# Sixteen k-tiles of an FFN's output projection as seven products of quarters, with weight sums formed by DMAs in scratch DRAM

## The chip, the cores and the metric

The kernel is one program on one core of a Trainium2 chip. The metric is device time in microseconds (us), lower is better. Engines are named as in the profile: PE (TensorE, matmuls), DVE (VectorE), ACT (ScalarE), POOL (GpSimd), SP (SyncE, which here only issues DMAs).

## The reference

A decoder trunk of two layers on 512 tokens of width 1024, in float32. Each layer has a token mixer, a cross-attention into 256 memory tokens and a SwiGLU FFN, each followed by a residual and a LayerNorm. What the change touches is the FFN, and the place where its weights are summed is the cross-attention:

```python
def swiglu(x, w_in, w_out):
    g, u = jnp.split(x @ w_in, 2, axis=-1)
    return (jax.nn.silu(g) * u) @ w_out
...
        h = layer_norm(DEEPNORM_ALPHA * h + mix, ln1_g[l], ln1_b[l])
        xa = memory_cross_attention(h, mem, w_xq[l], w_xkv[l], w_xo[l])
        h = layer_norm(DEEPNORM_ALPHA * h + xa, ln2_g[l], ln2_b[l])
        ff = swiglu(h, w_ffn_in[l], w_ffn_out[l])
        h = layer_norm(DEEPNORM_ALPHA * h + ff, ln3_g[l], ln3_b[l])
```

The hidden width of the FFN is 2816, which is 22 k-tiles of 128 for the output projection `w_out`.

## The kernel before

**Products.** Each float32 operand is kept as a high part (written by ACT, L101) and a low part (the rest, subtracted by DVE, L102). A product is three matmuls: high·high, high·low, low·high (L139 to L141). Every weight is loaded by a DMA that SP issues, in pieces of 128x1024 (512 KB), into one of four `raw` buffers, then split into a pair in `ring` or a `block`; `wchunk` (load at L125) does this for most of them.

**The FFN of one layer.** The 22 k-tiles are made in three parts of 8, 6 and 8. For each pair of k-tiles, `swiglu_seven` computes gate and up from the normalised input in seven products of quarters (a Strassen scheme; matmuls of 256 columns at L415 to L417, 168 of them per pair; only the first pair of a layer is made by `swiglu_plain`, 192 matmuls). Its weight sums are formed half by DVE and half by accumulating DMAs that POOL issues (`add_into`, L297). The result `sg` of 128x512 is split into `ph` and `pl`.

After each part, `out_proj` multiplies these k-tiles with their rows of `w_out`. For each of the four token tiles (`tt`, 128 tokens) it runs over the part's k-tiles and the two column halves of 512, three matmuls of 512 columns each, into two PSUM banks, and DVE adds the banks into the residual `h[tt]` (L286). The tile framework interleaves the matmuls of neighbouring token tiles.

**The end of a layer.** In the last part, each token tile is normalised as soon as it is complete, all on DVE: statistics (L290), mean and variance (L186, L188), subtract and scale (L192), a Newton iteration on 128x1 values (L149 to L162), scale and shift (L198). In layer 0, PE then transposes the tile (`lt_ln`, L206), ACT and DVE split it into `hT_ln`, and the next layer's first projection `pp_c` begins; it is computed in two halves, the first of which needs token tiles 0 and 1, the second tiles 2 and 3. Its weights `w_c` are split by DVE too. In layer 1, the tiles are stored instead, and the last token tile is computed in columns of 512, 256 and 256.

**Order.** Each engine runs its instructions in a fixed order, which the tile framework sets when the kernel is built, by simulating a timeline and by priorities (`tc.high_priority`). SP's DMAs stand in a queue of their own, where an issue waits until its buffer is free.

## Time and profile before

| | |
|---|---|
| median of 3 runs | 1428.9 us (1426.16 to 1429.18) |
| the profiled execution | 1427.96 us, of which the span of the trace is 1426.0 us |
| PE | 98% of the span busy, 8949 matmuls |
| DVE / ACT / POOL | 73% / 43% / 11% busy |
| the FFN of layer 0 | from 387.0 us to 722.7 us of the span |

The share of an engine is an average over the whole program; which engine ends a stretch is read from the rows of that stretch. The end of a matmul is modelled in the trace, and matmuls overlap, so the spacing of their starts says how fast PE goes.

### The profile page before, as it was taken

To read this page: it belongs to the slowest core of one execution; us is meant where nothing else is said; L and a number is where in the kernel's file an instruction comes from. 1 tells how busy PE (TensorE), PEld (TensorE's weight loads), DVE (VectorE), ACT (ScalarE), POOL (GpSimd) and SP (SyncE) were. 2 spreads that over 40 slices of the span, in tenths; PEclk is the share of its full clock that TensorE was granted. 3 is DMA by queue.
4 is the path that set the end of the run, shared out by engine and by line. 5 is a ranking of instruction groups with operands and counts; after the bars stand their busy time and mean duration, and the time that the engine had idled before them with its cause. 6 is when DMAs were issued, how large, how long until landed. Compare 5 with 4: busy or idle time off the path is not lost.

```text
span 1426.0 us, 22119 instructions
## 1 busy us (share of the span) xinstructions
PE 1396.7 (98%) x8949; PEld 1251.3 (88%) x8949; DVE 1034.0 (73%) x1701; ACT 608.0 (43%) x977; POOL 151.4 (11%) x98
## 2 busy tenths in 40 slices
PE   7998989999999999999999999999999999999997
PEld 6787888988899899899897889889889998989996
DVE  6699978656886376576769999685678764756667
ACT  5552461442456055255136235524525632534540
POOL 2373330000010000000013200000000000000000
PEclk9999999999999999999999999999999999999999
DMA  7522242322265364465242235512215663545531
GB/s 253 152 63 90 86 151 71 105 70 92 75 163 148 104 155 126 122 167 155 77 124 89 74 114 168 163 59 89 78 42 142 165 181 75 137 144 134 163 104 60
DMA packets 109306, 168.63 MB, mean 118 GB/s; under 512 B 7548, under 2 KB 82000, under 8 KB 109204
## 3 DMA queue, kind: packets, MB, share of 16 engines
q1 hardware_dynamic: 103156, 145.99, 31.9%
q0 software_dynamic: 5760, 20.97, 7.8%
q8 instruction: 70, 1.15, 0.3%
q14 instruction: 32, 0.26, 0.1%
q10 hardware_dynamic: 288, 0.26, 0.1%
HBM read 144.13 MB, written 2.10 MB: 103 GB/s over the span
## 4 chain that ended last, share of the span: by engine, by line
PE 85%; DVE 6%; issue 3%; ACT 3%; POOL 2%; DMA 1%; SPq 0%; DVEq 0%; POOLq 0%; ACTq 0%
PE po_fo L140 6%; PE po_fo L139 6%; PE po_fo L141 6%; PE fx L417 5%; PE fx L415 5%; PE fx L416 5%; PE fw L416 3%; PE fw L417 3%; PE fw L415 3%; DVE cv L611 3%; PE pp_xq L139 2%; PE pp_xq L140 2%; PE pp_xq L141 2%; PE po_xo L141 2%; PE po_xo L139 2%
## 5 line engine op out<-in xcount | busy, mean ns | idle before, releaser
L611 DVE SCALAR_TENSOR_TENSOR cv<-u,chan,cv 128x511 f32<-128x511 f32 (+29 forms) x240 | 159.6, 728 | 0.2
L140 PE MATMUL po_fo<-w_fo,ph 128*128 128x512 f32 (+1 forms) x360 | 138.2, 385 | 0.0
L141 PE MATMUL po_fo<-w_fo,pl 128*128 128x512 f32 (+1 forms) x360 | 137.6, 385 | 0.0
L297 POOL DMA_DIRECT2D s<-raw_a x40 | 34.8, 873 | 952.9 <-PE pp_f L141 473.8
L139 PE MATMUL po_fo<-w_fo,ph 128*128 128x512 f32 (+1 forms) x360 | 132.0, 385 | 0.0
L101 ACT ACTIVATE w_a<-raw_a 128x1024 fp32r<-128x1024 f32 x60 | 63.2, 1055 | 135.6 <-PE po_fo L141 110.2
L102 DVE TENSOR_TENSOR w_s<-s,w_s 128x1024 fp32r<-128x1024 f32 x80 | 97.3, 1220 | 28.3 <-ACT w_s L101 28.1
L101 ACT ACTIVATE w_s<-s 128x1024 fp32r<-128x1024 f32 x80 | 83.8, 1053 | 46.6 <-DMA s<-raw_a 33.6
L286 DVE SCALAR_TENSOR_TENSOR h<-h,po_fo 128x512 f32<-128x512 f32 (+1 forms) x49 | 32.6, 674 | 90.6 <-PE po_fo L141 90.6
L417 PE MATMUL fx<-T_ln,w_s 128*128 128x256 f32 x320 | 90.6, 283 | 0.0
L416 PE MATMUL fx<-T_ln,w_s 128*128 128x256 f32 x320 | 90.6, 283 | 0.0
L415 PE MATMUL fx<-T_ln,w_s 128*128 128x256 f32 x320 | 90.6, 283 | 0.0
L102 DVE TENSOR_TENSOR w_a<-raw_a,w_a 128x1024 fp32r<-128x1024 f32 x60 | 73.2, 1220 | 11.7 <-ACT w_a L101 10.5
L141 PEld LDWEIGHTS po_fo<-w_fo,pl 128*128 128x128 f32 x360 | 67.7, 188 | 13.2
L140 PEld LDWEIGHTS po_fo<-w_fo,ph 128*128 128x128 f32 x360 | 67.7, 188 | 13.0
L139 PEld LDWEIGHTS po_fo<-w_fo,ph 128*128 128x128 f32 x360 | 67.3, 188 | 12.9
L102 DVE TENSOR_TENSOR w_fo<-raw_fo,w_fo 128x1024 fp32r<-128x1024 f32 x44 | 52.9, 1219 | 16.2 <-ACT w_fo L101 16.2
L415 PEld LDWEIGHTS fx<-T_ln,w_s 128*128 128x128 f32 x320 | 61.4, 192 | 0.0
L416 PEld LDWEIGHTS fx<-T_ln,w_s 128*128 128x128 f32 x320 | 61.4, 192 | 0.0
L417 PEld LDWEIGHTS fx<-T_ln,w_s 128*128 128x128 f32 x320 | 61.4, 192 | 0.0
L140 PE MATMUL pp_xq<-hT_ln,w_xq 128*128 128x256 f32 (+1 forms) x192 | 61.3, 322 | 0.0
L139 PE MATMUL pp_xq<-hT_ln,w_xq 128*128 128x256 f32 (+1 forms) x192 | 60.0, 320 | 0.5 <-ACT hT_ln L101 0.5
(317 smaller groups left out, 4420.5 us busy)
## 6 DMA issues: line engine op xcount, KB each, us to landing
raw_a<-w_ffn_in SPq DMA_DIRECT2D x60, 512.0 KB
raw_fo<-w_ffn_out SPq DMA_DIRECT2D x44, 512.0 KB
s<-raw_a POOLq DMA_DIRECT2D x40, 512.0 KB, 5.1
s<-w_ffn_in SPq DMA_DIRECT2D x20, 512.0 KB
raw_xv<-w_xkv SPq DMA_DIRECT2D x16, 512.0 KB
raw_c<-w_in SPq DMA_DIRECT2D x16, 512.0 KB
...
```

Source lines behind the costliest of these rows:

```text
L101: ACT.activation(hi, src, AF.Copy)
L102: eng.tensor_sub(lo, src, f(hi))
L139: PE.matmul(o, lh, rh, start=start, stop=False)
L140: PE.matmul(o, lh, rl, start=False, stop=False)
L141: PE.matmul(o, ll, rh, start=False, stop=stop)
L286: DVE.scalar_tensor_tensor(h[tt][:, c0:c1], h[tt][:, c0:c1], scale, bks[c][:, :c1 - c0], ALU.mult, ALU.add)
L297: POOL.dma_start(dst, src, accum_op=ALU.add)
L415: PE.matmul(o, wh, bh, start=start and k == 0, stop=False, skip_group_check=True)
L416: PE.matmul(o, wh, bl, start=False, stop=False, skip_group_check=True)
L417: PE.matmul(o, wl, bh, start=False, stop=stop and k == 3, skip_group_check=True)
L611: DVE.scalar_tensor_tensor(cv[ct][:, s:], u[:, ct, :T - s], wj, cv[ct][:, s:], ALU.mult, ALU.add)
```

## The change

The parts become 8, 8 and 6 k-tiles. The first two, 16 k-tiles, use a new `out_proj_seven`; the last keeps `out_proj`, with its LayerNorms.

`out_proj_seven` takes the 8 k-tiles of a part as 4 pairs and splits the product into quarters: k-tiles of even and odd place, token halves of 256, column halves of 512. Seven products replace eight. Each is 2 token tiles x 4 pairs x 3 = 24 matmuls of 512 columns, 168 for a part where 192 stood. In place of two banks per token tile there are three pairs of banks (X, W, Y), and each product (for X, the growing sum) is added to or subtracted from the quarters of `h` where it belongs: 14 adds of 128x512 by DVE for each part instead of 8.

The moving side needs sums of quarters of `sg`: the class `PairQuads` lets DVE form T1 to T4 (256 columns wide) for each pair and splits them, in place of the plain split. The weight side needs four sums, S1 to S4. Each is formed in scratch DRAM, in two halves of 512 KB: SP issues a copy of one quarter of `w_out`, and POOL an accumulating DMA on top of it. In all, 14 operands of 512 KB are loaded and split for each part, where 8 were.

The 16 copies and 16 accumulating DMAs of a layer are put into the cross-attention: a list `aside` holds them, and each `wchunk` load there (8 of `w_xq`, 8 of `w_xo`) is followed in SP's queue by one copy.

```diff
+    aside = []
+
+    def behind(load):
+
+        if aside:
+            with tc.issue_after(load.ins):
+                aside.pop(0)()
+
     def wchunk(src, nk, ncol, name, resident=False, fine=False):
 
         raw = stage.tile([P, 1024], F32, tag="raw", name=f"raw_{name}")
         rv = raw.rearrange("p (k c) -> p k c", k=nk)
-        nc.sync.dma_start(rv, src.rearrange("(k p) c -> p k c", p=P))
+        behind(nc.sync.dma_start(rv, src.rearrange("(k p) c -> p k c", p=P)))
         if resident:
             w = block([P, 2, 1024], F32R, f"w_{name}")
         else:
...
-        POOL.dma_start(dst, src, accum_op=ALU.add)
+        POOL.dma_start(dst, src, accum_op=ALU.add, max_dma_last_dim=4096)
...
+    class PairQuads:
+        PLACE = {"11": (0, 4, 6, 10), "21": (1, 5, 7, 11), "22": (2, 3, 8, 9)}
+        SUMS = {"T1": 0, "T2": 1, "T4": 2, "T3": 3}
+        def __init__(self, j0, name):
+            self.j0 = j0
+            self.t = [block([P, 2, 4, 256], F32R, f"pT{i}_{name}") for i in range(4)]
+            self.b = [block([P, 2, 4, 256], F32R, f"pB{i}_{name}") for i in range(3)]
+        def get(self, n, i):
+            if n in self.SUMS:
+                t, e = self.t[i], self.SUMS[n]
+            else:
+                e = self.PLACE[n][i]
+                t, e = self.b[e // 4], e % 4
+            return t[:, 0, e, :], t[:, 1, e, :]
+        def second(self, j, sg, uu):
+            i = (j - self.j0) // 2
+            t3 = uu[1][:, 256:]
+            DVE.tensor_sub(t3, sg[1][:, 256:], sg[0][:, 256:])
+            split(*self.get("T3", i), t3)
+            split(*self.get("22", i), sg[1][:, 256:])
+        def first(self, j, sg, uu):
+            i = (j - self.j0) // 2
+            for m, n in enumerate(("11", "21")):
+                split(*self.get(n, i), sg[m][:, :256])
+            t1, t2, t4 = uu[0][:, :256], uu[0][:, 256:], uu[1][:, :256]
+            DVE.tensor_sub(t1, sg[0][:, :256], sg[0][:, 256:])
+            DVE.scalar_tensor_tensor(t2, t1, -1.0, sg[1][:, 256:], ALU.mult, ALU.subtract)
+            DVE.scalar_tensor_tensor(t4, t2, -1.0, sg[1][:, :256], ALU.mult, ALU.subtract)
+            split(self.t[i][:, 0, 0:2, :].rearrange("p e c -> p (e c)"),
+                  self.t[i][:, 1, 0:2, :].rearrange("p e c -> p (e c)"), uu[0])
+            split(*self.get("T4", i), t4)
+    def quarter_of(w, c, k, u):
+        v = w.rearrange("(q two p) c -> two p q c", two=2, p=P)
+        return v[k][:, 2 * u:2 * u + 2, c * 512:(c + 1) * 512]
+    def weight_sums(w, name):
+        s = {n: [dram.tile([P, 2, 512], F32, tag=f"{n}{u}_{name}", name=f"{n}{u}_{name}") for u in range(2)]
+             for n in ("S1", "S2", "S3", "S4")}
+        def step(n, at, plus, u):
+            nc.sync.dma_start(s[n][u], quarter_of(w, *at, u))
+            add_into(s[n][u], s[plus][u] if plus in s else quarter_of(w, *plus, u))
+        for n, at, plus in (("S3", (0, 0), (1, 0)), ("S2", (1, 1), "S3"), ("S1", (1, 0), (1, 1)), ("S4", (0, 1), "S2")):
+            for u in range(2):
+                aside.append(lambda n=n, at=at, plus=plus, u=u: step(n, at, plus, u))
+        return s
+    def out_proj_seven(w, sums, pq, name, scale):
+        A = {"11": (0, 0), "12": (0, 1), "22": (1, 1)}
+        def operand(n, u):
+            raw = stage.tile([P, 1024], F32, tag="raw", name=f"raw_{n}{u}_{name}")
+            src = sums[n][u] if n in sums else quarter_of(w, *A[n], u)
+            nc.sync.dma_start(raw.rearrange("p (k c) -> p k c", k=2), src)
+            wt = ring.tile([P, 2, 1024], F32R, tag="w", name=f"w_{n}{u}_{name}")
+            split(wt[:, 0, :], wt[:, 1, :], raw)
+            return wt
+        plan = (("S3", "T3", "W"), ("11", "11", "X"), ("12", "21", "Y"), ("S2", "T2", "X"), ("22", "T4", "W"),
+                ("S1", "T1", "X"), ("S4", "22", "X"))
+        tags = {"X": "acc", "W": "tr", "Y": "cv"}
+        ws, banks, seen = {}, {}, set()
+        for n, b, g in plan:
+            if g not in banks:
+                banks[g] = [bank(f"fo{g}{i}_{name}", tag=tags[g]) for i in range(2)]
+            ws[n] = [operand(n, u) for u in range(2)]
+        def add(t, c, g, i):
+            tt, cs = t * 2 + i, slice(c * 512, (c + 1) * 512)
+            k = scale if (tt, c) not in seen else 1.0
+            seen.add((tt, c))
+            with tc.high_priority(offset=HP):
+                DVE.scalar_tensor_tensor(h[tt][:, cs], h[tt][:, cs], k, banks[g][i], ALU.mult,
+                                         ALU.subtract if c else ALU.add)
+        reads = {"S3": (1, 1), "11": (0, 0), "12": (0, 0), "S2": (0, 1), "22": (0, 1), "S1": (1, 1), "S4": (1, 0)}
+        opened = set()
+        for n, b, g in plan:
+            bank_major = n in ("S1", "S4")
+            parts = [(i, u) for i in range(2) for u in range(2)] if bank_major else \
+                [(i, u) for u in range(2) for i in range(2)]
+            for i, u in parts:
+                for k in range(2):
+                    ph, pl = pq.get(b, u * 2 + k)
+                    ts_ = slice(i * P, (i + 1) * P)
+                    wh, wl = (ws[n][u][:, j, k * 512:(k + 1) * 512] for j in range(2))
+                    o, first = banks[g][i], (g, i) not in opened
+                    opened.add((g, i))
+                    last = n in ("S4", "22", "12") and u == 1 and k == 1
+                    PE.matmul(o, ph[:, ts_], wh, start=first, stop=False, skip_group_check=True)
+                    PE.matmul(o, ph[:, ts_], wl, start=False, stop=False, skip_group_check=True)
+                    PE.matmul(o, pl[:, ts_], wh, start=False, stop=last, skip_group_check=True)
+                if bank_major and u == 1:
+                    add(*reads[n], g, i)
+            if not bank_major:
+                for i in range(2):
+                    add(*reads[n], g, i)
...
+        quads = isinstance(dest, PairQuads)
         with tc.high_priority(offset=HP):
             for m in range(2):
                 ACT.activation(sg[m][:, hi], X[m][:, lo], AF.Silu)
+            if quads:
+                for m in range(2):
+                    DVE.scalar_tensor_tensor(sg[m][:, hi], sg[m][:, hi], -1.0, uu[m][:, hi], ALU.mult, ALU.mult)
+                dest.second(j, sg, uu)
         product(w4, t4, W, False, True)
-        out = []
         with tc.high_priority(offset=HP):
             for m in range(2):
                 DVE.tensor_add(uu[m][:, lo], W[m][:, lo], u2[m])
             for m in range(2):
-                DVE.scalar_tensor_tensor(sg[m], sg[m], -1.0, uu[m], ALU.mult, ALU.mult)
-                split(ph[:, i0 + m, :], pl[:, i0 + m, :], sg[m])
-                out.append((ph[:, i0 + m, :], pl[:, i0 + m, :]))
-        return out
+                s = lo if quads else slice(0, T)
+                DVE.scalar_tensor_tensor(sg[m][:, s], sg[m][:, s], -1.0, uu[m][:, s], ALU.mult, ALU.mult)
+            dest.first(j, sg, uu)
...
+        sums = [weight_sums(a["w_ffn_out"][l][g * NK * P:(g + 1) * NK * P, :], n_(f"fs{g}")) for g in range(2)]
...
-        for part, (j0, nj) in enumerate(((0, 8), (8, 6), (14, 8))):
-            pT = []
+        for part, (j0, nj) in enumerate(((0, 8), (8, 8), (16, 6))):
+            seven = part < 2
+            p = PairQuads(j0, n_(f"p{part}")) if seven else Pairs(j0, nj, n_(f"p{part}"))
             for j in range(j0, j0 + nj, 2):
-                if (j - j0) % 4 == 0:
-                    ph = block([P, 4, T], F32R, n_(f"ph{j}"))
-                    pl = block([P, 4, T], F32R, n_(f"pl{j}"))
-                if j == 0:
-                    pT += swiglu_plain(w_fi, quads, j, ph, pl, f"{l}")
-                else:
-                    pT += swiglu_seven(w_fi, quads, j, ph, pl, (j - j0) % 4, f"{l}")
-            norm = None
-            if part == 2:
-                gb3 = load_gb(a["ln3_g"][l], a["ln3_b"][l], n_("ln3"))
-                hT = new_hT(n_("ln3")) if l < L - 1 else None
-
-                def norm(tt, st):
-                    layer_norm(tt, st, gb3, n_("ln3"), hT,
-                               store=out[0, tt * P:(tt + 1) * P, :] if l == L - 1 else None)
-            out_proj(w_fo[j0 * P:(j0 + nj) * P, :], pT, n_(f"fo{part}"), ALPHA if part == 0 else 1.0, norm=norm,
-                     fin=part == 2 and l == L - 1)
+                (swiglu_seven if j else swiglu_plain)(w_fi, quads, j, p, f"{l}")
+            scale = ALPHA if part == 0 else 1.0
+            w_part = w_fo[j0 * P:(j0 + nj) * P, :]
+            if seven:
+                out_proj_seven(w_part, sums[part], p, n_(f"fo{part}"), scale)
+                continue
+            gb3 = load_gb(a["ln3_g"][l], a["ln3_b"][l], n_("ln3"))
+            hT = new_hT(n_("ln3")) if l < L - 1 else None
+
+            def norm(tt, st):
+                layer_norm(tt, st, gb3, n_("ln3"), hT,
+                           store=out[0, tt * P:(tt + 1) * P, :] if l == L - 1 else None)
+
+            out_proj(w_part, p.stat, n_(f"fo{part}"), scale, norm=norm, fin=l == L - 1)
```

SP's queue, at the loads of `w_xo` (`raw_xo`) in layer 0's cross-attention, before:

```order
L125 DMA raw_xo_2990<-w_xo 128x1024
L125 DMA raw_xo_2995<-w_xo 128x1024
L125 DMA raw_xo_3000<-w_xo 128x1024
L125 DMA raw_xo_3005<-w_xo 128x1024
L125 DMA raw_xo_3010<-w_xo 128x1024
```

The same place in the changed kernel (`S_fs` is a half of one of the sums):

```order
L134 DMA raw_xo_3024<-w_xo 128x1024
L460 DMA S_fs_0_2318<-w_ffn_out 256x1x512
L134 DMA raw_xo_3031<-w_xo 128x1024
L460 DMA S_fs_0_2319<-w_ffn_out 256x1x512
L134 DMA raw_xo_3038<-w_xo 128x1024
L460 DMA S_fs_0_2316<-w_ffn_out 256x1x512
```

Every load now has a copy of the same size behind it; the accumulating DMAs stand in POOL's queue.

DVE, at the end of layer 0, where the low parts of `hT_ln` are written; `lt_ln_01` is token tile 1, `h_102` and `h_103` are the rows of token tiles 2 and 3, and `w_c` are the next layer's weights. Before:

```order
L192 SCALAR_TENSOR_TENSOR h_102<-h_102,mv_ln_02_6764,gb_ln_0_6490 128x512 x2
L149 TENSOR_SCALAR y_ln_02_6770<-v_ln_02_6766 128x1
L102 TENSOR_TENSOR hT_ln_0_6495<-lt_ln_01_0_6694,hT_ln_0_6493 128x4x128
L102 TENSOR_TENSOR hT_ln_0_6496<-lt_ln_01_1_6702,hT_ln_0_6494 128x4x128
L156 TENSOR_SCALAR t_ln_02_6771<-y_ln_02_6770,v_ln_02_6766 128x1
L162 TENSOR_SCALAR y_ln_02_6770<-t_ln_02_6771,y_ln_02_6770 128x1
L156 TENSOR_SCALAR t_ln_02_6771<-y_ln_02_6770,v_ln_02_6766 128x1
L162 TENSOR_SCALAR s_ln_02_6772<-t_ln_02_6771 128x1
L286 SCALAR_TENSOR_TENSOR h_103<-h_103,po_fo_0_3_0_6795 128x512
L162 TENSOR_SCALAR y_ln_02_6770<-s_ln_02_6772,y_ln_02_6770 128x1
L290 BN_STATS st_fo_03_6845<-h_103 128x6
```

The changed kernel, from the same L192 rows of token tile 2 (there `h_104`; `h_105` is token tile 3, and the adds are at L295):

```order
L201 SCALAR_TENSOR_TENSOR h_104<-h_104,mv_ln_02_6964,gb_ln_0_6736 128x512 x2
L103 TENSOR_TENSOR hT_ln_0_6741<-lt_ln_00_0_6832,hT_ln_0_6739 128x4x128
L299 BN_STATS st_fo_03_7033<-h_105 128x6
L158 TENSOR_SCALAR y_ln_02_6970<-v_ln_02_6966 128x1
L103 TENSOR_TENSOR hT_ln_0_6742<-lt_ln_00_1_6840,hT_ln_0_6740 128x4x128
L103 TENSOR_TENSOR w_c_100_7095<-raw_c_100_7093,w_c_100_7095 128x1024
L103 TENSOR_TENSOR w_c_101_7100<-raw_c_101_7098,w_c_101_7100 128x1024
L165 TENSOR_SCALAR t_ln_02_6971<-y_ln_02_6970,v_ln_02_6966 128x1
L103 TENSOR_TENSOR w_c_110_7107<-raw_c_110_7105,w_c_110_7107 128x1024
L295 SCALAR_TENSOR_TENSOR h_105<-h_105,po_fo_0_3_1_6996 128x512
L103 TENSOR_TENSOR hT_ln_0_6741<-lt_ln_01_0_6906,hT_ln_0_6739 128x4x128
L103 TENSOR_TENSOR hT_ln_0_6742<-lt_ln_01_1_6914,hT_ln_0_6740 128x4x128
```

The low parts of token tile 1 stood ahead of the first add of token tile 3; they now stand behind its second add (the one shown) and behind three splits of `w_c`.

## Rows read from the trace of the kernel before

**Rows 1.** The page: the span, and each engine's busy time, share and instructions.
```profile
span 1426.0 us, 22119 instructions
PE 1396.7 (98%) x8949; PEld 1251.3 (88%) x8949; DVE 1034.0 (73%) x1701; ACT 608.0 (43%) x977; POOL 151.4 (11%) x98
```

**Rows 2.** Windows, layer 0's FFN: from:to, length, busy PE, PEld, DVE, ACT, POOL, clock, DMA, GB/s.
```profile
387.00:722.70 335.70, 335.60 (x2325) 314.30 (x2325) 224.34 (x300) 150.32 (x231) 18.42 (x21) 1.00 0.48 129
```

**Rows 3.** Timeline of PE inside an `out_proj`: start, duration; seven rows left out between.
```profile
480.02 0.39 PE L140 MATMUL po_fo<-w_fo,ph 128*128 128x512 f32 x1
...
482.06 0.39 PE L140 MATMUL po_fo<-w_fo,ph 128*128 128x512 f32 x1
```

**Rows 4.** Windows, the period of one pair in `swiglu_seven`.
```profile
534.00:554.16 20.16, 20.16 (x170) 20.16 (x170) 12.98 (x17) 11.53 (x20) 0.88 (x1) 1.00 0.47 129
```

**Rows 5.** Timeline of DVE within that period, idle time before a row in brackets.
```profile
543.75 0.42 DVE L462 TENSOR_TENSOR uu<-fw,u 128x256 f32<-128x256 f32 x1 [2.81 <-PE fw L417]
544.09 1.22 DVE L102 TENSOR_TENSOR w_s<-s,w_s 128x1024 fp32r<-128x1024 f32 x1
545.22 0.68 DVE L464 SCALAR_TENSOR_TENSOR sg<-sg,uu 128x512 f32<-128x512 f32 x1
545.82 0.41 DVE L462 TENSOR_TENSOR uu<-fw,u 128x256 f32<-128x256 f32 x1
```

**Rows 6.** Timeline of DVE at the end of layer 0.
```profile
692.33 1.37 DVE L286 SCALAR_TENSOR_TENSOR h<-h,po_fo 128x512 f32<-128x512 f32 x2 [5.17 <-PE po_fo L141]
...
699.28 1.41 DVE L198 SCALAR_TENSOR_TENSOR h<-h,y_ln,gb_ln 128x512 f32<-128x512 f32 x2
...
720.12 3.48 DVE L102 TENSOR_TENSOR w_c<-raw_c,w_c 128x1024 fp32r<-128x1024 f32 x3
```

**Rows 7.** Timeline of PE, the next layer's first matmul.
```profile
722.71 0.28 PE L139 MATMUL pp_c<-hT_ln,w_c 128*128 128x256 f32 x1
```

**Rows 8.** The chain that ended last, end of layer 0: start, duration, piece.
```profile
723.35 0.87 PE lt_ln L206 x8
...
736.39 0.74 PE pp_c L139 x4
```

**Rows 9.** Timeline of DVE at the end of layer 1.
```profile
1388.10 1.36 DVE L286 SCALAR_TENSOR_TENSOR h<-h,po_fo 128x512 f32<-128x512 f32 x2 [4.90 <-PE po_fo L141]
1389.38 1.28 DVE L290 BATCH_NORM_STATS2 st_fo<-h 128x6 f32<-128x512 f32 x2
...
1392.33 0.14 DVE L149 TENSOR_SCALAR y_ln<-v_ln 128x1 int32<-128x1 int32 x1
...
1394.44 0.69 DVE L286 SCALAR_TENSOR_TENSOR h<-h,po_fo 128x512 f32<-128x512 f32 x1 [0.60 <-PE po_fo L141]
...
1405.33 1.37 DVE L286 SCALAR_TENSOR_TENSOR h<-h,po_fo 128x512 f32<-128x512 f32 x2 [2.44 <-PE po_fo L141]
...
1411.44 0.69 DVE L286 SCALAR_TENSOR_TENSOR h<-h,po_fo 128x512 f32<-128x512 f32 x1 [0.37 <-PE po_fo L141]
...
1417.19 0.42 DVE L286 SCALAR_TENSOR_TENSOR h<-h,po_fo 128x256 f32<-128x256 f32 x1 [1.99 <-PE po_fo L141]
...
1421.35 1.67 DVE L198 SCALAR_TENSOR_TENSOR h<-h,y_ln,gb_ln 128x256 f32<-128x256 f32 x4
```

**Rows 10.** Timeline of SP's DMA issues in layer 0's cross-attention.
```profile
212.59 44.75 SPq L125 DMA_DIRECT2D raw_xq<-w_xq  x8
274.55 44.13 SPq L125 DMA_DIRECT2D raw_xo<-w_xo  x8
```

**Rows 11.** Timeline of ACT there, where the loads are first read.
```profile
289.00 1.06 ACT L101 ACTIVATE w_xo<-raw_xo 128x1024 fp32r<-128x1024 f32 x1 [1.75 <-issue]
...
332.26 3.92 ACT L101 ACTIVATE w_xo<-raw_xo 128x1024 fp32r<-128x1024 f32 x4
```

**Rows 12.** The page's DMA queues: packets, MB, share of 16 engines' span.
```profile
q1 hardware_dynamic: 103156, 145.99, 31.9%
q0 software_dynamic: 5760, 20.97, 7.8%
```

More of the change, by code (lines that the diff above doesn't have):

```diff
@@ L374, in swiglu_plain @@
                                 kh == 0 and k == 0, kh == 1 and k == 3)
-        out = []
         with tc.high_priority(offset=HP):
+            sg, uu = ([tmp.tile([P, T], F32, tag="t", name=f"{s}{j}{m}_{name}") for m in range(2)] for s in ("sg", "uu"))
             for m in range(2):
-                sg = tmp.tile([P, T], F32, tag="t", name=f"sg{j}{m}_{name}")
-                ACT.activation(sg, banks[0][m], AF.Silu)
-                DVE.tensor_mul(sg, sg, banks[1][m])
-                split(ph[:, m, :], pl[:, m, :], sg)
-                out.append((ph[:, m, :], pl[:, m, :]))
@@ L463, in swiglu_seven @@
             for m in range(2):
[L464 to L467 removed]
+                s = lo if quads else slice(0, T)
+                DVE.scalar_tensor_tensor(sg[m][:, s], sg[m][:, s], -1.0, uu[m][:, s], ALU.mult, ALU.mult)
+            dest.first(j, sg, uu)
     def mem_T(name):
```

20 lines of the change are left out of this document (16 added, 4 removed).

## The prediction

> **What bounds the kernel now.** I read first the page's shares: PE is busy 98% of the span, DVE 73%, the others less than half [rows 1]. Then the windows of the FFN, the stretch that the change rewrites: PE is busy for 335.6 of 335.7 us at a granted clock of 1.00, DVE for 224.3 [rows 2]. So matmuls taken out of this stretch shorten it one for one, until another engine is late. Third, the ends of the two layers, where one chain runs through LayerNorm on DVE: there I read DVE's timeline and the chain. Last, the cross-attention, where the new DMAs go: SP's issues against ACT's reads.
>
> **PE: what is removed.** A part of 8 k-tiles costs `out_proj` 4 x 8 x 2 x 3 = 192 matmuls of 512 columns, and `out_proj_seven` 7 x 24 = 168. Between two starts nine matmuls apart lie 2.04 us [rows 3]: 0.227 us each. The 24 saved are 5.44 us for a part, and four parts give 21.8 us. This is the ceiling. Dividing 22 k-tiles as 8, 8, 6 in place of 8, 6, 8 changes no other count.
>
> **DVE inside the parts.** Its prices, from the spacing of starts [rows 5]: 0.34 us for 256 columns, 1.13 for a split of 1024, 0.60 for 512. One pair's period on PE is 168 matmuls in 20.16 us, in which DVE works 12.98 [rows 4]; in other periods it also has two weight sums (estimate 2 x 1.13), so up to 15.2. Per pair the change adds three differences and one more for T3 (4 x 0.34), low parts of five pieces of 256 and one of 512 in place of two of 512 (1.7 + 0.6 - 1.2), and multiplies in halves (4 x 0.34 - 2 x 0.6): 2.6 us in all. That makes 17.8 of 20.16, so DVE fits with over 2 us left. In the row before the weight split DVE had waited 2.81 us for PE [rows 5]: such waits are the cover. Should the work come too late there, PE waits at its next bank, and nothing else hides it.
>
> For a part, `out_proj_seven` adds six more splits (6.8 us) and six adds (3.6) on DVE: 10.4 us, in a stretch of 168 x 0.227 = 38.1 us. DVE's total over the FFN rises from 224 to some 224 + 2 x 10.4 + 8 x 2.6 = 266, against 335.7 - 10.9 = 325 on PE: 82%. Each bank pair is added to `h` while PE runs another product (24 x 0.227 = 5.4 us, against 2 x 0.6 for the adds), except X from S1 to S4, where the product runs bank by bank to give half of that. For these handoffs I put 1 us over all four parts, nearer to the lower end because the adds are short beside a product; the bounds are 0 and 4.8 (the adds of one product, 1.2 us, bare once in each part).
>
> **The end of layer 0.** The last part now has 6 k-tiles, so nearly the whole saving of the layer falls after the first add of the last `out_proj`. Counted in issue order from the start of the FFN's output products, PE has run 401 matmuls at that add before (192 + 144 + 65), and 396 now (168 + 168 + 60; token tiles 0 and 1 are interleaved). So up to there only 5 x 0.227 = 1.1 us is saved. The rest, 43 matmuls or 9.7 us, should come between that add at 692.33 and the second half of `pp_c` at 736.39 [rows 6, 8]. There DVE sets the pace: until the low part of token tile 1, on which `pp_c` begins, the changed order puts eight adds, seven statistics, six and four passes of 512 columns (L192, L198), four low parts, three splits of `w_c` and two Newton chains before PE may go on. Neighbouring operations overlap by 0.08 (0.68 long, the next start 0.60 later [rows 5]), so a pair of adds of 1.37 costs 0.65 each, a pass 0.66 (1.41 for two), a split 1.13 (3.48 for three) [rows 6], a statistic 0.64 (1.28 for two) [rows 9]; a low part is 512 wide, 0.60. Eight adds 5.2, seven statistics 4.5, ten passes 6.6, four low parts 2.4, three splits 3.4, and the small operations, counted as three chains of 1.5 (1392.33 until the wait of 0.60 that ends at 1394.44 [rows 9]), 4.5: 26.6 us. PE has only 84 x 0.227 + 2 x 0.87 for transposes [rows 8] = 20.8 us to do until then. It waits 5.8 us, where before it came from the last product to `pp_c` at 722.71 without a wait [rows 7]. 9.7 - 5.8 = 3.9, and with the 1.1 **layer 0 gains 5.0 us** of its 10.9.
>
> **The end of layer 1.** From the first add at 1388.10 to the last pass (1421.35 + 1.67 = 1423.02) are 34.9 us, in which DVE waits for PE 0.60 + 2.44 + 0.37 + 1.99 = 5.4 us [rows 9]. So its own work is 29.5 us. PE after the change needs from that add 68 x 0.227 + 36 x 0.12 (a matmul of 256 columns: 20.16 / 168 [rows 4]) = 19.7 us: DVE is the longer by 10. The stretch becomes 29.5, which is 5.4 shorter; ahead of it 402 matmuls become 394, 1.8. **Layer 1 gains 7.2 us.**
>
> **Cross-attention: what is added.** SP issues eight loads of `w_xo` in 44.13 us and eight of `w_xq` in 44.75 [rows 10], 5.5 us apiece, paced by buffers coming free. From the first issue at 274.55 to ACT's read at 289.00 are 14.4 us; the last, issued by 318.7, is read as the last of four from 332.26 on, at about 335 [rows 10, 11]: slack of over 14 us. With each load now come a copy and an accumulate of 512 KB. By the queues, q0 (40 accumulates) took 7.8% of 1426 us, 2.8 us each of all 16 engines; q1 moved 145.99 MB in 31.9%, 1.6 us for 512 KB [rows 12]. Sum: 1.6 + 1.6 + 2.8 = 6.0. No row shows a copy or accumulate whose both sides lie in DRAM. Lower bound: overlap as good as no cost, below 5.5. Upper: both doubled, 1.6 + 3.2 + 5.6 = 10.4, less what is issued while loads wait. At 6.0 the queue falls 0.5 x 8 = 4 us behind within the eight loads, which the 14 us cover. I take nothing, near the rows. PE, DVE and ACT get no new work there, and POOL's 16 accumulates a layer stand on an engine that is 11% busy [rows 1].
>
> The Trainium skill, page "DMA: Bandwidth & Descriptors", section "Issuing engines are not separate DMA queues", says that DMAs of all issuing engines run on the same 16 DMA engines and interleave. By that rule, POOL's accumulates delay SP's loads though their queue is another one; it speaks against the change, and the first rival below is worked out that way. No row of before shows the two together in this stretch.
>
> **Sum.** 5.0 + 7.2 - 1 = 11.2 us. The profiled execution took 1427.96 (2 us more than its span), so 1416.8; the median of the runs is 0.9 above it. I say **1417.5**.
>
> **The rivals.**
> *The loads of cross-attention fall behind (slower).* With t us of all DMA engines for a load, a copy and an accumulate, the last `w_xo` load is late by 8 x (t - 5.5) less 12.8 of slack (14.4, a load of 1.6 us taken off). It cancels the 11.2 us, 5.6 for a layer, when t = 5.5 + 18.4/8 = 7.8. At t = 9.6, short of the upper bound, it is 20 us a layer, and the time 1417.5 + 40 = 1457.5. For it: an accumulate is nearly twice the price of a load, and a copy within DRAM is unseen. Against: slack is large, and the loads in the FFN share the DMA engines with accumulates at a share of 0.48 without PE waiting [rows 2]. Chance 0.09; from it comes most of "slower".
>
> *DVE is late inside the pairs.* 16 pair periods of `swiglu` feed `PairQuads` over both layers. If PE waits x us in each, x = 0.7 takes all the gain (1428); x = 0.35 gives 1422. The point is a DVE period over 20.2 us: 2.4 more than my 17.8. For it: the order of DVE is fixed, and a late operation holds back the next; against: waits such as 2.81 in one place [rows 5]. Chance 0.21 for 1421 to 1431.
>
> *The layer ends cost nothing.* If DVE does its late work in PE's shadow, all 21.8 us come but the 1 us: 1407. For it: the pieces of the chain at layer 0's end are PE's [rows 8]; against: the sums above. Chance 0.1 for 1406 to 1412.
>
> **How the numbers follow.** The forecast case, 1412 to 1421, holds 0.6; its width is that of the handoffs and of an error of 10% in the two sums on DVE. The range of 8 in 10 takes in part of both neighbours, 1408 to 1428; outside remain 0.04 of the third rival, 0.05 of the second and the first. A measurement tells from no change about 0.2%, that is below 1426.0 or above 1431.8. Faster: 0.6 + 0.1 + 0.1 of the second rival = 0.80; same: 0.08 of the second; slower: its remaining 0.03 and the first rival, 0.12.
>
> **What would show it.** Right: the out_proj of the first two parts shows 168 matmuls at 0.227 without gaps; PE waits some 5 to 6 us ahead of `pp_c` in layer 0, on a low part of `hT_ln`; DVE's last stretch in layer 1 has no wait for PE; `w_xo` is read on ACT as before. Wrong: PE gaps in `fw` or `fx` rows released by DVE; a gap in cross-attention ahead of `pp_xq` or `po_xo` released by ACT or a DMA; a `pp_c` that begins without a wait.

## The result and the profile after

The changed kernel took 1412.36 us (median of 4 runs, 1410.32 to 1414.95) against 1427.53 for the kernel before in the same comparison (4 runs, 1423.87 to 1429.18): a ratio of 0.9898, 95% interval 0.9871 to 0.9925, so 10.7 to 18.4 us faster. 1417.5 had been forecast, with 1408 to 1428 as range. The profiled execution is the slowest of the four runs (1414.95 us, span 1413.3); against the span of before it is 12.7 us shorter, and the accounts below go by the two profiled executions.

The page of the changed kernel, first the span and the engines, then the DMA queues (packets, MB, share of 16 engines' span), which answer to [rows 1, 12]:

```profile
span 1413.3 us, 22464 instructions
PE 1380.2 (98%) x8847; PEld 1235.4 (87%) x8847; DVE 1110.4 (79%) x1905; ACT 650.4 (46%) x1065; POOL 181.8 (13%) x130
q1 hardware_dynamic: 118388, 175.35, 38.0%
q0 software_dynamic: 12416, 37.75, 14.6%
```

Windows of the changed kernel (from:to, length, busy PE, PEld, DVE, ACT, POOL, clock, DMA share, GB/s): the FFN of layer 0, from the same matmul on as [rows 2]; a stretch of its first product of seven, with some matmuls of the neighbouring pairs; the `w_xo` loads of cross-attention.

```profile
387.72:716.10 328.38, 326.81 (x2277) 305.54 (x2276) 259.01 (x392) 170.99 (x275) 18.37 (x21) 1.00 0.54 151
467.40:503.20 35.80, 35.80 (x166) 29.95 (x165) 29.07 (x37) 14.66 (x17) 1.06 (x2) 1.00 0.70 213
276.00:321.00 45.00, 45.00 (x271) 39.89 (x269) 26.42 (x52) 22.91 (x49) 6.78 (x7) 1.00 0.96 258
```

PE has no gap in the product of seven. DVE is busy for 79% of the FFN's stretch (259.0 of 328.4). The stretch of [rows 2] does not hold the whole FFN: in the kernel before its first matmul starts at 374.4, 12.6 us ahead of the 387.0 given there, and the accounts below start with that matmul. In cross-attention the DMA engines are now nearly full, 0.96, and PE is still busy for all of it.

To place the 12.7 us, the program is cut at points that both kernels have: the first matmul of the FFN (`pp_f`), the first transpose `pc` behind the start of the second half of `pp_c` (layer 0) and the last instruction (layer 1), read from PE's timeline.

| | layer 0, `pp_f` to `pc` | layer 1, `pp_f` to the end |
|---|---|---|
| before | 374.4 to 737.1: 362.7 us | 1070.2 to 1425.9: 355.7 us |
| changed | 375.1 to 733.7: 358.6 us | 1066.5 to 1413.2: 346.7 us |
| difference | 4.1 | 9.0 |

Outside of these the difference is 0.4 us the other way. So of the 10.9 us of matmuls that a layer saves, layer 0 keeps 4.1 and layer 1 keeps 9.0.

**Layer 0's end.** PE's timeline of the changed kernel, where `pp_c` begins (start, duration, idle before and its releaser):

```profile
716.11 0.62 PE L148 MATMUL pp_c<-hT_ln,w_c 128*128 128x256 f32 x3 [0.25 <-ACT hT_ln L102]
718.21 0.39 PE L148 MATMUL pp_c<-hT_ln,w_c 128*128 128x256 f32 x1 [1.48 <-DVE h L295]
718.81 0.39 PE L149 MATMUL pp_c<-hT_ln,w_c 128*128 128x256 f32 x1 [0.21 <-DVE hT_ln L103]
```

DVE's timeline just before, with everything that PE waits for in a row:

```profile
713.89 2.35 DVE L103 TENSOR_TENSOR w_c<-raw_c,w_c 128x1024 fp32r<-128x1024 f32 x2
716.16 0.27 DVE L165 TENSOR_SCALAR t_ln<-y_ln,v_ln 128x1 f32<-128x1 f32 x1
716.35 1.21 DVE L103 TENSOR_TENSOR w_c<-raw_c,w_c 128x1024 fp32r<-128x1024 f32 x1
717.48 0.68 DVE L295 SCALAR_TENSOR_TENSOR h<-h,po_fo 128x512 f32<-128x512 f32 x1
718.08 1.28 DVE L103 TENSOR_TENSOR hT_ln<-lt_ln,hT_ln 128x512 fp32r<-128x512 f32 x2
```

The reader sees the forecast queue: three splits of `w_c`, the second add of token tile 3, and only then the low parts. The longer wait, 1.48 us, ends with that add and not with a low part: `pp_c` and `po_fo` take their PSUM banks from the same four (`BANKS` in the kernel), and `pp_c`'s next high·high matmul needs the bank that the add reads. The low part ends the shorter one; it stands right behind the add, so an earlier add alone would have freed PE for one matmul only. PE's starts lie 1.76 and 0.60 us apart at the two matmuls where 0.12 is normal: 2.1 us lost. A second price follows, which no row of before shows. Windows of the changed kernel behind this wait:

```profile
718.80:722.70 3.90, 3.89 (x20) 3.89 (x21) 3.59 (x10) 1.67 (x3) 0.00 (x0) 0.58 0.47 129
722.70:726.70 4.00, 4.00 (x35) 4.00 (x34) 3.89 (x12) 0.00 (x0) 0.00 (x0) 0.99 0.91 285
```

The granted clock is 0.58 over 3.9 us (from 719.4 on PE is at the lower of its two levels, 1.2 GHz, 0.21 us per matmul where 0.12 is normal), then full again. In 3.9 us 20 matmuls start, in the next 4.0 there are 35. Sixteen at 0.09 more are 1.5 us.

**Layer 1's end.** DVE's last stretch, as in [rows 9]; of the rows between only those are shown in which DVE waits for PE, and the start of the last chain:

```profile
1383.14 1.28 DVE L295 SCALAR_TENSOR_TENSOR h<-h,po_fo 128x512 f32<-128x512 f32 x2 [5.13 <-PE po_fo L150]
...
1389.06 0.14 DVE L158 TENSOR_SCALAR y_ln<-v_ln 128x1 int32<-128x1 int32 x1
1389.11 0.69 DVE L299 BATCH_NORM_STATS2 st_fo<-h 128x6 f32<-128x512 f32 x1
1389.71 0.26 DVE L165 TENSOR_SCALAR t_ln<-y_ln,v_ln 128x1 f32<-128x1 f32 x1
1389.88 0.20 DVE L195 BATCH_NORM_AGGREGATE mv_ln<-st_fo 128x2 f32<-128x12 f32 x1
...
1400.94 0.42 DVE L295 SCALAR_TENSOR_TENSOR h<-h,po_fo 128x256 f32<-128x256 f32 x1 [0.62 <-PE po_fo L150]
...
1403.09 0.42 DVE L295 SCALAR_TENSOR_TENSOR h<-h,po_fo 128x256 f32<-128x256 f32 x1 [0.45 <-PE po_fo L150]
...
1407.08 0.15 DVE L158 TENSOR_SCALAR y_ln<-v_ln 128x1 int32<-128x1 int32 x1
...
1408.63 1.67 DVE L207 SCALAR_TENSOR_TENSOR h<-h,y_ln,gb_ln 128x256 f32<-128x256 f32 x4
```

From the first add to the last pass 27.2 us (1383.14 to 1410.30), where before it was 34.9. The waits for PE shrank from 5.4 to 1.1. The rest, 3.4 us, is something else: now that DVE has two token tiles at hand, the small operations of one chain stand between operations of another tile (1389.06 to 1389.88), whereas the last chain, alone, still takes 1.55 us (1407.08 to 1408.63). The same stretch as windows of the kernel before:

```profile
1388.10:1423.02 34.92, 29.06 (x151) 24.85 (x149) 28.18 (x69) 0.00 (x0) 0.00 (x0) 0.97 0.13 49
```

And of the changed kernel:

```profile
1383.14:1410.30 27.16, 19.91 (x105) 17.03 (x103) 25.78 (x69) 0.00 (x0) 0.00 (x0) 0.91 0.17 62
```

69 instructions on DVE each time; 28.2 us of busy time became 25.8. Summed one by one they are hardly shorter (30.6 and 30.3 us); what grew is the time in which one overlaps the next (2.4 and 4.6 us).

**Inside the parts.** In layer 0 PE loses 3.2 us more than before ahead of the last products (the sum over the starts of what exceeds 0.227 and 0.120 us), in layer 1 0.5. In this execution it is mostly in the first part, ahead of `fx`. ACT there stands behind an accumulating DMA:

```profile
408.65 1.06 ACT L102 ACTIVATE w_s<-s 128x1024 fp32r<-128x1024 f32 x1 [4.89 <-DMA s<-raw_a]
```

But ACT's timeline of before has the same wait at the same place (33.4 us behind the FFN's first matmul, 33.5 after), and PE loses nothing there:

```profile
407.80 1.06 ACT L101 ACTIVATE w_s<-s 128x1024 fp32r<-128x1024 f32 x1 [4.77 <-DMA s<-raw_a]
```

So the late DMA alone does not make PE wait. New are the splits of `PairQuads` on ACT behind it. The longest of these waits shows one, in ACT's timeline of the changed kernel:

```profile
434.05 0.61 ACT L102 ACTIVATE pT_p<-uu 128x512 fp32r<-128x512 f32 x1
434.57 0.37 ACT L564 ACTIVATE u<-fx 128x256 f32<-128x256 f32 x1
```

And in PE's:

```profile
434.99 0.39 PE L551 MATMUL fx<-T_ln,w_s 128*128 128x256 f32 x1 [0.51 <-ACT u L564]
```

PE waits for the copy `u`, and the new split delays that copy by 0.52 us.

### The profile page after: what moved, and what is told of

It reads as the page before. It is cut to its first block, busy times and chain, and to the rows that moved or that the text cites. A ratio compares the mean times of both kernels' runs of the same rounds, so it can differ in the third digit from the quotient of the medians.

```text
span 1413.3 us, 22464 instructions
## 1 busy us (share of the span) xinstructions
PE 1380.2 (98%) x8847; PEld 1235.4 (87%) x8847; DVE 1110.4 (79%) x1905; ACT 650.4 (46%) x1065; POOL 181.8 (13%) x130
## 4 chain that ended last, share of the span: by engine, by line
PE 87%; DVE 3%; ACT 3%; issue 3%; POOL 2%; DMA 1%; SPq 0%; DVEq 0%; ACTq 0%; POOLq 0%
PE fx L551 5%; PE fx L553 5%; PE fx L552 5%; PE fw L553 3%; PE fw L552 3%; PE fw L551 3%; PE pp_xq L149 2%; PE pp_xq L148 2%; PE pp_xq L150 2%; PE foX_fo L512 2%; PE po_xo L150 2%; PE po_xo L148 2%; PE foX_fo L513 2%; PE po_xo L149 2%; PE foX_fo L514 2%
## 5 line engine op out<-in xcount | busy, mean ns | idle before, releaser
L103 DVE TENSOR_TENSOR w_s<-s,w_s 128x1024 fp32r<-128x1024 f32 x80 | 97.6, 1220 | 38.9 <-ACT w_s L102 38.7
L149 PE MATMUL pp_xq<-hT_ln,w_xq 128*128 128x256 f32 (+1 forms) x192 | 61.3, 322 | 0.0
L148 PE MATMUL pp_xq<-hT_ln,w_xq 128*128 128x256 f32 (+1 forms) x192 | 59.9, 320 | 0.5 <-ACT hT_ln L102 0.5
L150 PE MATMUL pp_xq<-hT_ln,w_xq 128*128 128x256 f32 (+1 forms) x192 | 60.4, 318 | 0.0
L102 ACT ACTIVATE hT_ln<-lt_ln 128x512 fp32r<-128x512 f32 x24 | 13.9, 595 | 97.5 <-PE lt_ln L215 97.3
L149 PE MATMUL pp_c<-hT_ln,w_c 128*128 128x512 f32 (+1 forms) x160 | 56.9, 358 | 0.2 <-DVE hT_ln L103 0.2
L148 PE MATMUL pp_c<-hT_ln,w_c 128*128 128x512 f32 (+1 forms) x160 | 55.1, 361 | 1.7 <-DVE h L295 1.5
L150 PE MATMUL pp_c<-hT_ln,w_c 128*128 128x512 f32 (+1 forms) x160 | 56.3, 354 | 0.0
L102 ACT ACTIVATE w_S_fo<-raw_S_fo 128x1024 fp32r<-128x1024 f32 x32 | 33.8, 1058 | 35.8 <-PE foX_fo L514 14.2
L149 PE MATMUL po_xo<-w_xo,oTh 128*128 128x512 f32 x128 | 49.5, 389 | 0.0
L150 PE MATMUL po_xo<-w_xo,oTl 128*128 128x512 f32 x128 | 49.4, 391 | 0.0
```

The lines of the kernel that those rows point to most:

```text
L102: ACT.activation(hi, src, AF.Copy)
L103: eng.tensor_sub(lo, src, f(hi))
L148: PE.matmul(o, lh, rh, start=start, stop=False)
L149: PE.matmul(o, lh, rl, start=False, stop=False)
L150: PE.matmul(o, ll, rh, start=False, stop=stop)
```

## The experiments

All spans are those of the profiled execution. The two stretches are cut as in the table above. What lies outside of them takes 702.8 to 708.3 us in these executions (705.3 and 703.7 in the two of one and the same kernel, with `w_c` on POOL), so not all of a difference between two spans belongs to the FFN.

| run | us, median (range) | span | layer 0 stretch | layer 1 stretch |
|---|---|---|---|---|
| split only | 1429.93 (1429.24 to 1431.24) | 1428.2 | 364.8 | 357.1 |
| one part | 1417.47 (1416.22 to 1418.22) | 1416.2 | 359.4 | 352.1 |
| 8, 6, 8 | 1419.07 (1414.95 to 1422.16) | 1415.2 | 360.0 | 352.5 |
| no token sums | 1409.82 (one run) | 1408.1 | 355.9 | 347.2 |
| no weight sums | 1412.45 (1412.01 to 1414.61) | 1410.9 | 355.1 | 349.0 |
| weight sums twice | 1440.75 (1439.46 to 1442.94) | 1441.2 | 370.3 | 364.5 |
| `w_c` on POOL | 1411.60 (1411.18 to 1412.90) | 1409.5 | 356.7 | 347.5 |
| 6, 8, 8 | 1420.24 (1419.75 to 1422.09) | 1418.0 | 361.0 | 350.9 |
| changed, again | 1413.58 (1411.00 to 1416.88) | 1415.2 | 358.0 | 348.8 |
| `w_c` on POOL, again | 1409.76 (1407.98 to 1410.52) | 1406.3 | 355.0 | 347.5 |

### The split into 8, 8, 6 alone

In the kernel before:

```diff
-        for part, (j0, nj) in enumerate(((0, 8), (8, 6), (14, 8))):
+        for part, (j0, nj) in enumerate(((0, 8), (8, 8), (16, 6))):
```

> The kernel before with its parts as 8, 8 and 6 k-tiles, all by the plain output projection: no matmul less, no sums. Theory (the last part's size decides what the end of a layer costs): the last part is 6 k-tiles as in the changed kernel, so PE waits about 3.6 us for DVE at the end of layer 0, and at the end of layer 1 DVE's stretch is 7.7 us shorter while 42 matmuls (9.5 us) more come ahead of it, 1.8 us longer. Sum: 5.4 us slower than before, a span near 1431. Rival (the loss comes with the seven products, from their adds and splits on DVE): no change, a span near 1426, and no wait of PE at pp_c.

Measured: 1.0034 of before (interval 1.0022 to 1.0046), so 3.1 to 6.6 us slower; by the stretches 2.1 in layer 0 and 1.4 in layer 1. PE's timeline at `pp_c` has the wait of the changed kernel to 0.01 us:

```profile
722.37 0.62 PE L139 MATMUL pp_c<-hT_ln,w_c 128*128 128x256 f32 x3 [0.25 <-ACT hT_ln L101]
724.47 0.38 PE L139 MATMUL pp_c<-hT_ln,w_c 128*128 128x256 f32 x1 [1.48 <-DVE h L286]
725.08 0.39 PE L140 MATMUL pp_c<-hT_ln,w_c 128*128 128x256 f32 x1 [0.22 <-DVE hT_ln L102]
```

The clock stayed at 1.00 behind it, and so layer 0 lost 2.1 and not 3.6. The theory holds: the wait comes from the last part's six k-tiles, not from the seven products. Set against this run, the products alone give 6.2 us in layer 0 and 10.4 in layer 1, of 10.9 each; the rest is what was found above, 3.2 of waits inside the parts and 1.5 of clock in layer 0, 0.5 of waits in layer 1. DVE's last stretch in layer 1 is 27.2 us here too (1398.10 to 1425.26), so its shortening comes from the split as well.

### One part by seven products

```diff
-        for part, (j0, nj) in enumerate(((0, 8), (8, 8), (16, 6))):
-            seven = part < 2
+        for part, (j0, nj) in enumerate(((0, 8), (8, 6), (14, 8))):
+            seven = part == 0
...
+            if part == 1:
+                out_proj(w_part, p.stat, n_(f"fo{part}"), scale)
+                continue
```

> The parts stay 8, 6, 8; only the first part of each layer uses the seven products (8 copies and 8 accumulates a layer in place of 16). 48 matmuls less, 10.9 us. Theory (ends cost what the last part's size makes them cost, and the first part loses 3.2 us in layer 0 and 0.5 in layer 1 inside its pairs): ends as before, 1426.0 - 10.9 + 3.7 = 1418.8 span. Rival (every part of seven products pays its own share of the loss, half of 9.1 us): 1426.0 - 10.9 + 4.5 with waits inside the pairs small and a wait at the layer end: 1419.6; the two are told apart by where PE waits, not by the time. Third, no loss: 1415.

Measured: 0.9943 of before (0.9930 to 0.9956); the stretches are 3.3 and 3.6 us shorter, of 5.4 each. `pp_c` begins without a wait, as before:

```profile
717.02 0.39 PE L150 MATMUL po_fo<-w_fo,p_p 128*128 128x512 f32 x1
717.25 0.28 PE L148 MATMUL pp_c<-hT_ln,w_c 128*128 128x256 f32 x1
```

A last part of 8 costs nothing at the end. The 2 us missing in each layer are waits ahead of `fx` in the first part (in layer 0 PE's starts there exceed the normal spacing by 0.37, 0.36 and 0.30 in single places). So the waits inside the pairs were not 3.2 and 0.5 as in the one profile of the changed kernel, but about 2 in both layers of this execution.

### Parts of 8, 6 and 8, the first two by seven products

The second part has three pairs; its second halves are 256 KB. The core of the edit:

```diff
-        for part, (j0, nj) in enumerate(((0, 8), (8, 8), (16, 6))):
+        for part, (j0, nj) in enumerate(((0, 8), (8, 6), (14, 8))):
...
+        sizes = (2, w.shape[0] // (2 * P) - 2)
...
-                for k in range(2):
+                for k in range(sizes[u]):
```

> The parts stay 8, 6, 8, and the first two use the seven products, the second with three pairs (126 matmuls in place of 144); the last part of 8 is plain. 84 matmuls less than before in all (19.0 us), 12 more than in the changed kernel (2.7 us). Theory (a last part of 8 k-tiles leaves PE the longer engine at the layer's end): the ends cost what they cost before, and of the 19.0 only the waits inside the pairs are lost, about 3.7: span 1410.7, 2.6 less than the changed kernel. Rival (ends cost nothing that depends on the split; what counts is the number of matmuls): 2.7 more than the changed kernel, 1416.

Measured: 0.9956 of before (0.9940 to 0.9973): slower than the changed kernel, against the theory, and not for the rival's reason either. The end of layer 0 has no wait, as forecast, but a new wait stands at the head of the third part. PE's timeline there:

```profile
597.09 0.28 PE L557 MATMUL fx<-T_ln,w_s 128*128 128x256 f32 x1
600.97 0.58 PE L555 MATMUL fx<-T_ln,w_s 128*128 128x256 f32 x1 [3.60 <-ACT u L568]
```

ACT's timeline of the same run:

```profile
599.59 1.06 ACT L102 ACTIVATE w_s<-s 128x1024 fp32r<-128x1024 f32 x1 [7.07 <-DMA s<-raw_a]
600.55 0.37 ACT L568 ACTIVATE u<-fx 128x256 f32<-128x256 f32 x1
```

And POOL's:

```profile
592.37 1.77 POOL L306 DMA_DIRECT2D s<-raw_a  x2 [10.88 <-DMA raw_a<-w_ffn_in]
```

PE waits for ACT's copy `u`, which frees its bank; the copy stands on ACT behind a weight split, that behind an accumulating DMA of `swiglu_seven`, and POOL issued this late because a load of `w_ffn_in` came late. Behind the wait the clock is 0.61 for 4 us. In layer 1 the waits at this place add up to 3.4 us.

### Parts of 6, 8 and 8

The same with the part of three pairs first.

> As the run with parts 8, 6, 8, but 6, 8, 8: three pairs first, the last part of 8 again plain, so the same matmuls. There PE waited 3.8 and 3.4 us in the first pair behind the three-pair product, for an accumulating DMA. Theory (the three-pair product is too short to hide the loads and sums of the next pair's weights): the waits of 3 us and more move to the head of the second part, and the head of the third, behind a full product, has none; the time stays within 2 us of that run. Rival (it is the third part, with a plain product next, that is short of buffers): the waits stay at the head of the third part. Third: no such wait, 7 us faster than that run.

Measured: 0.9958 of before (0.9943 to 0.9973), 1.2 us from the run above. The wait moved to the head of the second part (PE in layer 0):

```profile
481.20 0.28 PE L557 MATMUL fx<-T_ln,w_s 128*128 128x256 f32 x1
485.09 0.58 PE L555 MATMUL fx<-T_ln,w_s 128*128 128x256 f32 x1 [3.61 <-ACT u L568]
```

and there is none of over 0.3 us at the head of the third, behind a product of four pairs. The theory holds as far as the place goes: the wait stands behind the product of three pairs, wherever that is. That it is the length of this product which decides, 28.6 us of PE work (126 matmuls) with three pairs or 38.1 (168) with four, because the loads of the next pair need that time, is argued and not shown; the product of three pairs also has smaller second halves. So the last part of 8, which cures the end of the layer, has a price here: six k-tiles then go through the seven products.

### Without the sums on the moving side

T1 to T4 are not formed; the products read the quarters of `sg` instead, so this part of the computation is left out:

```diff
-            if n in self.SUMS:
-                t, e = self.t[i], self.SUMS[n]
-            else:
-                e = self.PLACE[n][i]
-                t, e = self.b[e // 4], e % 4
+            e = self.PLACE[{"T1": "11", "T2": "21", "T4": "11", "T3": "22"}.get(n, n)][i]
+            t, e = self.b[e // 4], e % 4
```

> The changed kernel without the sums on the moving side: T1 to T4 are not formed or split, and the products read quarters of sg in their place, so the output is left wrong by that much. DVE loses 2.6 us and ACT 1.3 us for each pair. Theory (the waits in the first part come from DVE and ACT being late behind this work): PE's waits of 3.2 us in layer 0's first part go to under 0.5, span near 1410. Rival (they come from an accumulating DMA that lands late, whatever DVE does): the waits in front of fx stay at 2 us or more, and the span stays above 1412.

Measured: one run, 1409.82 us, span 1408.1; layer 0's first part has no wait of PE. That looks like the theory, but the changed kernel's second profile (below) has none in that part either, so this place does not tell the two apart. Layer 1 took 347.2, no less than the changed kernel's 346.7. Summed over all parts of both layers, PE's starts lose 1.3 us more than before here, 3.7 and 5.2 in the changed kernel's two profiles, and 2.7 to 4.5 in the three other profiles with the same parts and token sums (no weight sums, `w_c` on POOL twice). That speaks for the theory, but it is one execution.

### Without the weight sums

```diff
-            src = sums[n][u] if n in sums else quarter_of(w, *A[n], u)
+            src = quarter_of(w, *A.get(n, (1, 0)), u)
```

The copies and accumulating DMAs are gone, and quarters of the weights stand in for the sums, so this part of the computation is left out.

> The changed kernel without its copies and accumulating DMAs: where a sum S1 to S4 is wanted, a quarter of the weights is loaded, so the output is wrong by that much. Theory (the sums lie under PE's work in cross-attention): the same time within 2 us, cross-attention as long as with them, and the DMA share between 276 and 321 us falls from 0.96 to about 0.27. Rival (the nearly full DMA engines cost something that the spans hide): 3 us or more faster, with shorter waits ahead of pp_xq or po_xo.

Measured: 1412.45 us, 0.9904 of before (0.9889 to 0.9919), the same as with the sums. Windows at the `w_xo` loads:

```profile
276.00:321.00 45.00, 45.00 (x267) 39.81 (x266) 26.88 (x53) 22.38 (x48) 0.00 (x0) 1.00 0.27 91
```

The DMA share is back at 0.27, and PE is as busy. The sums cost nothing that can be measured; the interval leaves some 2 us either way.

### The weight sums twice

```diff
             add_into(s[n][u], s[plus][u] if plus in s else quarter_of(w, *plus, u))
+            nc.sync.dma_start(again[n][u], quarter_of(w, *at, u))
+            add_into(again[n][u], quarter_of(w, *at, u))
```

> The changed kernel with every copy and every accumulate twice, the second pair into scratch that nobody reads. A load, a copy and an accumulate took 1.5 + 1.5 + 3.0 us of all DMA engines in the changed kernel; with doubled sums 10.5 for each load, in a place where 5.5 us pass between loads. Theory of the prediction's first rival (work on the DMA engines adds up, and beyond 7.8 us a load it costs time): 8 x (10.5 - 5.5) - 12.8 = 27 us a layer, a span near 1413 + 54 = 1467. Other theory (only the sums fall behind, the loads keep their place): within 5 us of the changed kernel.

Measured: 1440.75 us, 1.0101 of before (1.0086 to 1.0116), 28 us slower than the changed kernel: between the two theories, and at a place that neither named. PE's cross-attention is as long as ever (`pp_xq` 253.5 to 314.2 us, 60.7 as in the changed kernel). Then PE stands still in the FFN, by its timeline:

```profile
422.28 0.58 PE L555 MATMUL fx<-T_ln,w_s 128*128 128x256 f32 x1 [12.40 <-ACT u L568]
```

ACT's timeline of this run:

```profile
419.68 1.06 ACT L102 ACTIVATE w_s<-s 128x1024 fp32r<-128x1024 f32 x1 [18.02 <-DMA s<-raw_a]
```

And POOL's, from its first accumulate of the layer:

```profile
219.07 1.20 POOL L306 DMA_DIRECT2D S_fs<-w_ffn_out  x1 [3.95 <-DMA S_fs<-w_ffn_out]
...
410.70 1.05 POOL L306 DMA_DIRECT2D xS_fs<-w_ffn_out  x1 [5.78 <-issue]
413.13 0.91 POOL L306 DMA_DIRECT2D s<-raw_a  x1 [1.38 <-issue]
```

The 32 accumulating DMAs go out on POOL from 219.07 to 410.70, one in 6.2 us, and the FFN's own first accumulate stands behind them in the same queue. In the changed kernel the 16 are done long before, by POOL's timeline:

```profile
220.42 1.23 POOL L306 DMA_DIRECT2D S_fs<-w_ffn_out  x1 [3.24 <-DMA S_fs<-w_ffn_out]
...
326.21 0.83 POOL L306 DMA_DIRECT2D S_fs<-S_fs  x1 [2.92 <-DMA S_fs<-w_ffn_out]
399.22 0.90 POOL L306 DMA_DIRECT2D s<-raw_a  x1 [72.19 <-PE pp_f L150]
```

There POOL waits 72 us for the FFN: some eleven more accumulates a layer would fit (an estimate, 72 by 6.2).

### Two splits of `w_c` on POOL

```diff
-        wlo_engines(DVE)
+        wlo_engines(*((DVE,) if l == 0 else (POOL, DVE)))
```

> The changed kernel with every other low part of layer 1's first w_c pieces on POOL (two of the four at the layer's end). Theory (at the end of layer 0 PE waits because DVE has the splits of w_c between the LayerNorm and the low part of hT): PE's waits of 1.6 and 0.5 us inside pp_c go, 1 to 2 us faster than the changed kernel. Rival (POOL needs 2.4 us for what takes DVE 1.1, and PE waits for that): the same waits, released by POOL, no gain.

Measured: 1411.60 us, 0.9898 of before (0.9881 to 0.9914). Since that is within the changed kernel's range, both ran once more, on one chip:

> The changed kernel once more, beside the next run on the same chip. Theory (its losses in layer 0's first part come from accumulating DMAs whose landing differs from run to run): about 1412, a span between 1408 and 1414; PE's wait at the end of layer 0, which no DMA sets, is again 1.6 + 0.5 us inside pp_c. Rival (both are fixed by the order): the same waits to 0.1 us in both places.

> The kernel with two of the four low parts of w_c on POOL, again, to be set against the changed kernel on the same chip. Theory (two splits off DVE at the end of layer 0): 1 to 2 us faster than the changed kernel, about 1411. Rival (POOL's slower splits give it back): the same time.

Measured: the changed kernel 1413.58 (0.9912 of before, 0.9897 to 0.9928), with POOL 1409.76 (0.9887, 0.9871 to 0.9902). The ranges of the runs do not meet (1407.98 to 1410.52, and 1411.00 to 1416.88); 3.8 us lie between the medians, where the first pair of runs had 0.8. PE's timeline at `pp_c`, in the second run with POOL:

```profile
709.60 0.62 PE L148 MATMUL pp_c<-hT_ln,w_c 128*128 128x256 f32 x3 [0.25 <-ACT hT_ln L102]
710.56 0.39 PE L148 MATMUL pp_c<-hT_ln,w_c 128*128 128x256 f32 x1 [0.34 <-DVE h L295]
711.28 0.39 PE L149 MATMUL pp_c<-hT_ln,w_c 128*128 128x256 f32 x1 [0.33 <-DVE hT_ln L103]
```

The window behind it:

```profile
711.20:715.00 3.80, 3.72 (x31) 3.73 (x32) 3.80 (x12) 1.26 (x2) 0.76 (x1) 1.00 0.45 98
```

The wait of 1.48 is 0.34, the next one grew from 0.21 to 0.33 (0.50 and 0.60 us over the normal spacing), and the clock stays at 1.00 behind them. The changed kernel's second profile has its wait again (1.62 and 0.48 us over the normal spacing, where the first had 1.64 and 0.48) and its clock at 0.68 for 3.9 us. So the wait at the layer's end is fixed by the order on DVE. From the first add of the last part to `pc`, layer 0 takes:

| | us | clock behind the wait |
|---|---|---|
| changed kernel, both profiles, and no token sums | 38.9 | 0.58, 0.68, 0.64 |
| split only, and no weight sums | 37.4 | 1.00 |
| `w_c` on POOL, both profiles | 36.9 | 1.00 |

So the edit is worth 1.9 us here, as forecast, and 1.5 of it is the clock that does not fall; the waits got shorter but did not go. The rest of the 3.8 us is not explained by it: of the 8.9 us between the spans of the two second profiles, 4.6 lie outside both stretches. By medians this version is the fastest that computes the whole result.

The waits inside the parts are not fixed: in the changed kernel's second profile they add up to 2.6 us more than before in layer 0 again (3.4 against 0.8 over the normal spacing), but in other places: 0.5 inside the first product of seven, 0.6 and 0.9 at the heads of the second and the third part. In layer 1 they are 2.6 as well, where the first profile had 0.5.

## Why the prediction was right

1412.4 lies in the range, at the fast edge of the forecast case (1412 to 1421). The gain was 15.2 us by the medians and 12.7 between the two profiled executions, where 11.2 had been forecast. The mechanism, savings cut down at the layers' ends, was right; the two ends were both mis-sized, and partly it is luck that the sum came near.

**The matmuls.** 21.8 us for four parts, at 0.227 us apiece: right; the 672 matmuls of the four products start 0.227 us apart, and their window shows PE without a gap.

**DVE in the parts.** 266 us were forecast for the stretch of [rows 2], 259 measured; 79% of it, 82% forecast. The adds into `h` at the bank handoffs delayed nothing in the first profile, and 0.5 us in one place of layer 0 in the second. The allowance of 1 us for this over all parts was too small, and in the wrong place: it is inside the pairs that PE waits, 3.2 and 0.5 us in the first profile, 2.6 and 2.6 in the second, about 2 in each layer in the run with one part. The second rival (DVE late inside the pairs, 0.7 us in each period to cancel the gain) came true at a third to a half of that (3.7 or 5.2 us in 16 periods), but the engine that PE waits for is nearly always ACT, not DVE, and ACT's new splits were not priced. For the stronger case of the three-pair product the rows show a late accumulating DMA ahead of a split on ACT. For the changed kernel they show a new split ahead of the copy that PE waits for in the longest of its waits, and the one run without token sums agrees; the shares of late DMAs and of new splits in the whole loss stay open.

**The end of layer 0.** The place was right, and so was the queue on DVE; the run with the split alone shows both. But the longer part of the wait is for a bank, which the second add of token tile 3 frees, and only the shorter one for the low part that was named. The size was put together from errors. DVE's queue through the low parts of token tile 1 takes 24.5 us (694.86 to 719.36) and not 26.6, and PE goes on with the first of these two, after 23.9; PE itself comes after 21.3 and not 20.8, and has four matmuls (0.6 us) that it can run. So it waits 2.1 us and not 5.8; but PE's clock then falls, 1.5 us more. That these and the waits inside the parts left the forecast gain nearly standing is luck. Layer 0 was to gain 5.0 less some of the allowance of 1 and gained 4.1: 1.8 us were lost up to the first add of the last products (6 fewer matmuls give 1.4, the waits take 3.2) and 5.9 gained after it.

**The end of layer 1.** The term that was mis-sized: 7.2 us forecast, 9.0 measured. DVE's own work was taken as 29.5 us because before it had that length without the waits for PE. But part of this length was one small operation waiting for the one before, and that part closes when another token tile's operations stand between: 26.1 us (27.2 less 1.1). That DVE would have no wait for PE left was wrong too, by these 1.1 us. Layer 0's sum on DVE counts its small operations at the same price and was too long as well; how much of its 2.1 us comes from that was not measured.

**Cross-attention.** Nothing was forecast and nothing came. Over 213 to 335 us in the changed kernel, the two queues took 43.1% and 39.1% of 16 engines' time; 16 accumulates in 39.1% of 122 us are 3.0 us each, where 2.8 were put. By the Trainium skill, page "DMA: Bandwidth & Descriptors", section "Issuing engines are not separate DMA queues", all these DMAs share 16 engines; the share of 0.96 agrees with it. What that cost was nothing here: no read of `w_xq` or `w_xo` by ACT or DVE waits for a DMA, in the changed kernel or with doubled sums.

**The rival on the other side** named the right resource at the wrong point. With doubled sums, 10.5 us a load, the loads of `w_xo` were not late by the 27 us that its formula gives; it is the accumulates on POOL that fall behind, and PE pays 12.4 us in layer 0 and 12.1 in layer 1 for it, in the FFN, and with its clock (0.57 over the 4 us behind the wait in layer 0).
